# Three RMS norms with reciprocal root and scaled rows in PSUM, and the last chunk of two MLP first blocks with the contraction outermost

## The chip, the cores and the metric

The kernel runs on one core of one Trainium2 chip. The time is the device time of one execution in microseconds (us), read as the median of several executions. The engines are TensorE (PE in the rows, its weight loads PEld), VectorE (DVE), ScalarE (ACT), GpSimd (POOL) and SyncE (SP, here the queue that issues most DMAs). PSUM holds the results of matmuls: 8 banks of 128 partitions by 512 fp32 values.

## What is computed

A two-layer diffusion trunk on 1024 latent tokens and 256 context tokens of width 1024. Layer 0 mixes with a convolution and a Fourier transform, layer 1 with neighbourhood attention; each layer ends with a squared-ReLU MLP of width 4096. Ahead of every sub-layer stands an RMS norm with a shift and a scale:

```python
def _rms(x, g):
    y = x * lax.rsqrt(jnp.mean(x * x, axis=-1, keepdims=True) + EPS)
    return y * g
def _modulate(h, shift, scale):
    return h * (1 + scale) + shift
def _mlp(h, w1, w2):
    return jnp.square(jax.nn.relu(h @ w1)) @ w2
# per layer: x = x + gate1 * mixer(_modulate(_rms(x, g1), shift1, scale1))
#            x = x + gate2 * _mlp(_modulate(_rms(x, g2), shift2, scale2), w1, w2)
# ctx goes the same way with its own modulation (in the last layer it only feeds the attention)
```

## The kernel before

The token stream is kept transposed in SBUF as `xT[dt][ci]`: 8 blocks of 128 channels (`dt`) by 3 chunks of tokens (`ci`): chunks 0 and 1 are 512 latent tokens each, chunk 2 the 256 context tokens. Every dense product is done in three matmuls on numbers split into a high and a low part (`mm3`, L293 to L296): high by high, high by low, low by high. `dense` (L298) makes one block of 128 outputs for one chunk: 8 channel blocks `kt` by 3 matmuls, 24 in all, into one PSUM bank. `partial_groups` (L314) makes the output projections in groups of 6 or 12 matmuls; `residual` (L311, DVE) adds each group to `xT`, and `done` then squares the new block for the next norm.

The class `Norm` (L357) works in three steps. `square`: ACT squares each block (L369, L372) and DVE, or POOL where the caller says so, adds it to a sum in SBUF (L373). `stat`: a matmul with ones (L383) sums over the partitions, DVE takes mean plus epsilon out of PSUM (L386), ACT makes a first reciprocal root (L352) and DVE improves it in three instructions (L353 to L355); the result `y` is an SBUF tile named `ny`. `out`, once for each `dt`: on even blocks DVE forms x*g*y in an SBUF tile (L400), ACT adds the shift and writes the high part (L401), DVE the low part (L402); on odd blocks POOL multiplies x by y (L407), ACT does scale and shift (L405) and the copy to the high part (L406), DVE the low part (L408). The parts are called `mh`, `ml` ahead of the MLPs and `ah`, `al` ahead of the attention.

Three such norms are touched. I call their places **stage 1** (about 395 to 486 us, ahead of the first MLP), **stage 2** (about 1300 to 1375 us, ahead of the q, k, v projections, whose matmuls stand at L1152 to L1154) and **stage 3** (about 2005 to 2075 us, ahead of the second MLP). In each the norm of the chunk that is finished first is interleaved with the output projection of another chunk by `close_stream`, and the chunk that is finished last (`late`: chunk 0 in stage 1, chunk 1 in stage 3) gets its statistic and its eight `out` calls in the middle of the first block of the MLP (`mlp`, fc = 0): behind the first of the three dense groups of the chunk before it. The weights come by DMA as fp32 and are split into high and low by ACT (L247) and POOL or DVE (L248). The squared ReLU of an MLP group is L963 and L965 (ACT), L966 (POOL) and L967 (DVE).

All PSUM tiles come from one pool of 8 banks (`bank`). A scheduler assigns each tile a bank in the order in which the program asks for it, and orders the instructions of each engine; an engine waits where a tile's bank is not yet free.

Of the kernel before, what the change touches and what calls it, by code (L numbers as in the profile page):

```python
# [8 lines left out]
F32 = mybir.dt.float32  # L9
F32R = mybir.dt.float32r  # L10
BF16 = mybir.dt.bfloat16
AF = mybir.ActivationFunctionType
ALU = mybir.AluOpType
# [4 lines left out]
P = 128  # L18
D = 1024
DT = 8  # L20
# [3 lines left out]
EPS = 1e-6  # L24
CHUNKS = [(0, 512, 0), (512, 512, 0), (1024, 256, 1)]
# [11 lines left out]
def trunk(ctx: ExitStack, tc, x_t, cx_t, vecs, cc, ada, ada_t, w_in, w_out_2, w_fold, w_32, mlp_w1, mlp_w2, w_qkv, na_w_out_2, na_w_out_4, bias_pad,  # L37
# [4 lines left out]
    pp = ctx.enter_context(tc.tile_pool(name="pp", bufs=1))  # L42
# [20 lines left out]
    def bank():  # L63
        return psp.tile([P, 512], F32, tag="ps", name="ps")
# [64 lines left out]
    def tmp(dt=F32):  # L129
        return bp.tile([P, 512], dt, tag="tmp", name="tmp", bufs=ntmp[0])  # L130
# [219 lines left out]
    def rsqrt_newton(v, y, t):  # L350
# [3 lines left out]
                lambda: DVE.tensor_tensor(out=t, in0=t, in1=v, op=ALU.mult),  # L354
                lambda: DVE.scalar_tensor_tensor(out=y, in0=t, scalar=1.5, in1=y, op0=ALU.add, op1=ALU.mult)]  # L355

    class Norm:  # L357


        def __init__(self, l, k, hi, lo, room=None):  # L360
            self.l, self.k, self.hi, self.lo = l, k, hi, lo
            self.acc, self.y = {}, {}
            self.room = room or (lambda ci, which: keep())

# [14 lines left out]
        def stat_steps(self, ci, ps=None):  # L379
            w = CHUNKS[ci][1]  # L380
            if ps is None:
                ps = bank()
                PE.matmul(ps[:, :w], lhsT=ones, rhs=self.acc[ci][:, :w], start=True, stop=True)  # L383
            v, y, t = (a[:, :w] for a in (tmp(), self.room(ci, 1), tmp()))
            self.y[ci] = y
            return [lambda: DVE.tensor_scalar(out=v, in0=ps[:, :w], scalar1=1.0 / D, scalar2=EPS, op0=ALU.mult, op1=ALU.add)] + rsqrt_newton(v, y, t)  # L386
# [5 lines left out]
        def out_steps(self, dt, ci, on_dve=None):  # L392
            off, w, s = CHUNKS[ci]
            g = gtile[self.l][self.k][:, dt, s:s + 1]
            sh = mods[self.l][:, 24 * self.k + dt, s:s + 1]
            x, y, a = xT[dt][ci], self.y[ci], tmp()[:, :w]
            hs = self.hi[dt][:, off:off + w]
            ls = self.lo[dt][:, off:off + w]
            if dt % 2 == 0 if on_dve is None else on_dve:
                return (lambda: DVE.scalar_tensor_tensor(out=a, in0=x, scalar=g, in1=y, op0=ALU.mult, op1=ALU.mult),  # L400
                        lambda: ACT.activation(hs, a, AF.Identity, bias=sh),  # L401
                        lambda: DVE.scalar_tensor_tensor(out=ls, in0=a, scalar=sh, in1=hs.bitcast(F32), op0=ALU.add, op1=ALU.subtract))  # L402

            def high():
                ACT.activation(a, a, AF.Identity, bias=sh, scale=g)  # L405
                ACT.copy(hs, a)  # L406
            return (lambda: POOL.tensor_tensor(out=a, in0=x, in1=y, op=ALU.mult), high,  # L407
                    lambda: DVE.tensor_tensor(out=ls, in0=a, in1=hs.bitcast(F32), op=ALU.subtract))  # L408
# [458 lines left out]

    m_hi = [big(f"mh{d}") for d in range(DT)]
    m_lo = [big(f"ml{d}") for d in range(DT)]
    norm = Norm(0, 1, m_hi, m_lo)  # L870

    sequence(0, 0)
    sequence(1, 0)
# [72 lines left out]
        for t in todo:  # L946
            t()

    gs = partial_groups(y_hi[2:4], y_lo[2:4], 0, 0, (0,), 2, done=lambda m, ci: norm.square(m, ci, POOL if m % 2 else DVE))
    close_stream(gs[:4], gs[4:], (1,), norm)  # L950


    def mlp(l, norm, cis, late, fill, end, nf=8):
# [1 line left out]
        hh, hl = norm.hi, norm.lo  # L955

        def up(pcs, ci, uh, ul, between=None):
            off, w, _ = CHUNKS[ci]
            ps = dense(pcs, ci, hh, hl)
            if between:  # L960
                between()
            r, q = tmp(), tmp()
            ACT.activation(r[:, :w], ps[:, :w], AF.Relu)  # L963
            hs = uh[:, off:off + w]
            ACT.activation(hs, r[:, :w], AF.Square)  # L965
            POOL.tensor_tensor(out=q[:, :w], in0=r[:, :w], in1=r[:, :w], op=ALU.mult)  # L966
            DVE.tensor_tensor(out=ul[:, off:off + w], in0=q[:, :w], in1=hs.bitcast(F32), op=ALU.subtract)  # L967

        order = [ci for ci in cis if ci != late] + [late]
        for fc in range(nf):  # L970
# [3 lines left out]
            if fc == 0:  # L974
                pcs = take()
                pcs += [w for a in plan.pop(0) for w in pieces(*a, lambda: big("wq")[:, 0:1024])]
                for n, ci in enumerate(order):
                    for i in range(3):
                        w = pcs[2 * i:2 * i + 2]
                        if (n, i) == (1 - l, 0):  # L980
                            up(w, ci, uh[i], ul[i], lambda: norm.stat(late))
                            norm.all_out(late)
                        else:
                            up(w, ci, uh[i], ul[i])
                f = 3
            while f < 4:
                pcs = take()
# [11 lines left out]

    a_hi = []  # L1000
    a_lo = []
    norm1 = Norm(1, 0, a_hi, a_lo)

    def end0(uh, ul):
        a_hi.extend(big(f"ah{d}") for d in range(DT))
# [313 lines left out]
    for i in range(len(seq) + 3):  # L1319
# [21 lines left out]
        if 3 <= i:  # L1341
# [7 lines left out]
    slot[0], ntmp[0] = NLAT, 5  # L1349
    m_hi = [big(f"mh{d}") for d in range(DT)]  # L1350
    m_lo = [big(f"ml{d}") for d in range(DT)]
    norm = Norm(1, 1, m_hi, m_lo)
    close_stream(partial_groups(o_hi[6:], o_lo[6:], 1, 0, (0,), 2, done=norm.square, lag=3),
                 partial_groups(o_hi[4:], o_lo[4:], 1, 0, (1,), 4, done=lambda m, ci: norm.square(m, ci, POOL if m % 2 else DVE)), (0,), norm, wait=2)

# [299 lines left out]
```

## Time and profile before

| what | us |
|---|---|
| median of 3 runs | 2735.89 (2733.70 to 2740.11) |
| the profiled execution, its own time | 2737.96 |
| its span in the trace | 2736.1 |
| PE busy in the span | 2638.0 |

The profiled execution lies 2.1 us above the median. PE is busy for 96% of the span, so the time is read as PE's busy time plus PE's idle time, and the question for each stage is what PE waits for there and at which clock it runs afterwards.

### The profile page before, as it was taken

What the parts mean: (1) busy time and instruction counts of PE and PEld (TensorE: products, weight loads), DVE (VectorE), ACT (ScalarE), POOL (GpSimd) and SP (SyncE); (2) the same over time, 40 slices, a digit from 0 to 9 for tenths busy, and PEclk for the clock granted to TensorE, in tenths of its full rate; (3) what the DMA queues carried; (4) which work ended last, traced back from release to release, by engine and by line L of the source; (5) the groups of instructions that cost most, each with busy time, mean ns of one, the idle gap of its engine ahead of it and who ended that gap; (6) DMA issues with size and microseconds to landing.
All of it is one profiled execution on the core that took longest, in us unless ns stands there. A gap on an engine that the chain in (4) does not pass through costs nothing.

```text
span 2736.1 us, 37282 instructions
## 1 busy us (share of the span) xinstructions
PE 2638.0 (96%) x13787; PEld 2186.3 (80%) x13787; DVE 1665.2 (61%) x3623; ACT 913.9 (33%) x1988; POOL 1017.1 (37%) x838
## 2 busy tenths in 40 slices
PE   7989799999999999999899999999989899999999
PEld 5878687888888888888688887788868778788787
DVE  5778779455464554624962535888877645545545
ACT  4211246121221211213532225766744232232322
POOL 3323256332332322323411002544466454454543
PEclk9999899999999999999999999999999999999999
DMA  7233420222222222311333334534221111111112
GB/s 251 72 115 124 132 82 16 63 92 81 81 96 73 85 84 78 97 43 46 97 119 116 122 118 138 166 101 136 92 66 39 39 60 48 47 55 39 62 46 85
DMA packets 148937, 239.44 MB, mean 88 GB/s; under 512 B 10460, under 2 KB 91644, under 8 KB 148756
## 3 DMA queue, kind: packets, MB, share of 16 engines
q1 hardware_dynamic: 147316, 234.45, 26.8%
q8 instruction: 108, 1.77, 0.3%
q10 hardware_dynamic: 1440, 2.62, 0.2%
q14 instruction: 73, 0.60, 0.1%
HBM read 208.71 MB, written 28.32 MB: 87 GB/s over the span
## 4 chain that ended last, share of the span: by engine, by line
PE 72%; DVE 9%; issue 3%; DMA 2%; POOL 2%; ACT 1%; DVEq 0%; POOLq 0%; SPq 0%; ACTq 0%
PE ps L295 16%; PE ps L294 16%; PE ps L296 16%; PE ps L1464 5%; PE ps L1152 3%; PE ps L1154 3%; PE ps L1153 3%; PE ps L102 3%; PE ps L1288 3%; DMA raw<-in_mlp_w_dram 2%; PE ps L1105 2%; DVE junk L218 1%; POOL wsp L248 1%; PE ps L1107 1%; DVE ny L373 1%
## 5 line engine op out<-in xcount | busy, mean ns | idle before, releaser
L248 POOL TENSOR_TENSOR wsp<-raw,wsp 128x512 fp32r<-128x512 f32 x355 | 500.0, 1413 | 938.0 <-ACT wsp L247 904.4
L311 DVE SCALAR_TENSOR_TENSOR xT<-ps,mods,xT 128x512 f32<-128x512 f32 x528 | 367.0, 711 | 308.8 <-PE ps L296 308.3
L247 ACT CAST wsp<-raw 128x512 fp32r<-128x512 f32 x368 | 224.5, 619 | 758.6 <-PE ps L296 538.7
L295 PE MATMUL ps<-ul,wsp 128*128 128x512 f32 (+1 forms) x1280 | 473.5, 370 | 1.7 <-DVE ul L1470 0.8
L218 DVE CUSTOM_DVE_ANT_0 junk<-raw,cond_b 128x256 bf16<-128x256 f32 x640 | 354.8, 554 | 192.6 <-DMA raw<-in_ada_t_dram 92.7
L296 PE MATMUL ps<-uh,wsp 128*128 128x512 f32 (+1 forms) x1280 | 468.4, 368 | 0.0
L294 PE MATMUL ps<-uh,wsp 128*128 128x512 f32 (+1 forms) x1280 | 458.9, 369 | 0.5 <-ACT wsp L247 0.5
L295 PE MATMUL ps<-ml,wsp 128*128 128x512 f32 (+1 forms) x792 | 285.5, 361 | 11.1 <-DVE ml L408 7.5
L294 PE MATMUL ps<-mh,wsp 128*128 128x512 f32 (+1 forms) x792 | 284.6, 361 | 1.2 <-ACT mh L401 1.2
L296 PE MATMUL ps<-mh,wsp 128*128 128x512 f32 (+1 forms) x792 | 283.7, 359 | 0.0
L295 PEld LDWEIGHTS ps<-ul,wsp 128*128 128x128 f32 x1280 | 241.4, 189 | 47.0 <-DVE ul L1470 7.2
L294 PEld LDWEIGHTS ps<-uh,wsp 128*128 128x128 f32 x1280 | 241.4, 189 | 41.9 <-ACT wsp L247 0.9
L296 PEld LDWEIGHTS ps<-uh,wsp 128*128 128x128 f32 x1280 | 241.2, 188 | 40.0
L966 POOL TENSOR_TENSOR tmp<-tmp 128x512 f32<-128x512 f32 (+1 forms) x104 | 103.8, 999 | 217.8 <-ACT tmp L963 189.6
L295 PEld LDWEIGHTS ps<-ml,wsp 128*128 128x128 f32 x792 | 151.1, 191 | 37.4 <-DVE ml L408 10.8
L294 PEld LDWEIGHTS ps<-mh,wsp 128*128 128x128 f32 x792 | 151.0, 191 | 24.6 <-ACT mh L401 1.4
L296 PEld LDWEIGHTS ps<-mh,wsp 128*128 128x128 f32 x792 | 151.2, 191 | 21.4
L1464 PE MATMUL ps<-mh,wsp 128*128 128x512 f32 x448 | 148.1, 397 | 14.0 <-ACT ny L1481 7.2
L963 ACT ACTIVATE tmp<-ps 128x512 f32<-128x512 f32 (+1 forms) x104 | 55.3, 532 | 257.7 <-PE ps L296 257.2
L967 DVE TENSOR_TENSOR ul<-tmp,uh 128x512 fp32r<-128x512 f32 (+1 forms) x104 | 90.5, 875 | 80.8 <-POOL tmp L966 80.8
L294 PE MATMUL ps<-hh,wsp 128*128 128x512 f32 (+1 forms) x360 | 130.0, 361 | 1.9 <-ACT wsp L247 1.6
L295 PE MATMUL ps<-hl,wsp 128*128 128x512 f32 (+1 forms) x360 | 129.5, 360 | 2.0 <-DVE hl L408 1.3
(335 smaller groups left out, 5079.0 us busy)
## 6 DMA issues: line engine op xcount, KB each, us to landing
raw<-in_mlp_w_dram SPq DMA_DIRECT2D x92, 512.0 KB, 3.5
raw<-in_ada_t_dram SPq DMA_DIRECT2D x80, 512.0 KB, 3.5
raw<-in_mlp_w_dram SPq DMA_DIRECT2D x80, 256.0 KB, 2.7
raw<-in_w_qkv_dram SPq DMA_DIRECT2D x24, 512.0 KB, 4.0
k_d<-tmp SPq DMA_DIRECT2D x40, 256.0 KB, 2.4
kh<-k_d SPq DMA_DIRECT2D x15, 640.0 KB, 5.0
kl<-k_d SPq DMA_DIRECT2D x15, 640.0 KB, 6.9
araw<-in_ada_dram SPq DMA_DIRECT2D x16, 512.0 KB, 9.6
```

Of the source, the lines that this page charges most:

```text
L102: PE.transpose(dst, src, ident[:rows, :rows])
L218: DVE.tensor_tensor_reduce(out=junk, in0=raw[:, d * 256:d * 256 + 256], in1=cond_b[:, s, :], op0=ALU.mult, op1=ALU.add, scale=1.0, scalar= ...
L247: ACT.copy(dst_hi, src)
L248: lo_eng.tensor_tensor(out=dst_lo, in0=src, in1=dst_hi.bitcast(F32), op=ALU.subtract)
L294: PE.matmul(ps, lhsT=whi, rhs=ahi, start=first, stop=False)
L295: PE.matmul(ps, lhsT=whi, rhs=alo, start=False, stop=False)
L296: PE.matmul(ps, lhsT=wlo, rhs=ahi, start=False, stop=last)
L311: DVE.scalar_tensor_tensor(out=xT[dt][ci], in0=ps, scalar=mods[l][:, 24 * k + 16 + dt, s:s + 1], in1=xT[dt][ci], op0=ALU.mult, op1=ALU.add)
L966: POOL.tensor_tensor(out=q[:, :w], in0=r[:, :w], in1=r[:, :w], op=ALU.mult)
L967: DVE.tensor_tensor(out=ul[:, off:off + w], in0=q[:, :w], in1=hs.bitcast(F32), op=ALU.subtract)
L1152: PE.matmul(ps, lhsT=ah, rhs=wh, start=(kt == 0), stop=False)
L1464: PE.matmul(ps, lhsT=a, rhs=b, start=(first and kt == 0 and n == 0), stop=(kt == 3 and n == 2), skip_group_check=True)
```

## The change

The three norms get `psum=True`. Their statistic then goes straight from the PSUM bank of the ones matmul into ACT (scale 1/D, bias from a new tile `eps`, L391 of the changed kernel), DVE needs three instructions (L392 to L394) and not four, and `y` is written to a PSUM bank. Each `out` takes the DVE form for all eight blocks; x*g*y goes to a PSUM bank (L411), ACT reads it there (L412), DVE makes the low part (L413). POOL no longer multiplies (L407) or adds squares (L373). In the first block of both MLPs the late chunk runs its three dense groups together, in three open banks, with `kt` in the outer loop; the three squared ReLUs follow.

```diff
+    eps = pp.tile([P, 1], F32, name="eps")
+    POOL.memset(eps, EPS)
...
+            if self.psum:
+                y, y0, t = bank()[:, :w], tmp()[:, :w], tmp()[:, :w]
+                self.y[ci] = y
+                return [lambda: ACT.activation(y0, ps[:, :w], AF.Abs_reciprocal_sqrt, scale=1.0 / D, bias=eps),
+                        lambda: DVE.scalar_tensor_tensor(out=t, in0=y0, scalar=-0.5 / D, in1=y0, op0=ALU.mult, op1=ALU.mult),
+                        lambda: DVE.scalar_tensor_tensor(out=t, in0=ps[:, :w], scalar=D * EPS, in1=t, op0=ALU.add, op1=ALU.mult),
+                        lambda: DVE.scalar_tensor_tensor(out=y, in0=t, scalar=1.5, in1=y0, op0=ALU.add, op1=ALU.mult)]
...
-            x, y, a = xT[dt][ci], self.y[ci], tmp()[:, :w]
+            x, y, a = xT[dt][ci], self.y[ci], (bank if self.psum else tmp)()[:, :w]
...
-            if dt % 2 == 0 if on_dve is None else on_dve:
+            if self.psum or (dt % 2 == 0 if on_dve is None else on_dve):
...
-    norm = Norm(0, 1, m_hi, m_lo)
+    norm = Norm(0, 1, m_hi, m_lo, psum=True)
...
-    gs = partial_groups(y_hi[2:4], y_lo[2:4], 0, 0, (0,), 2, done=lambda m, ci: norm.square(m, ci, POOL if m % 2 else DVE))
+    gs = partial_groups(y_hi[2:4], y_lo[2:4], 0, 0, (0,), 2, done=norm.square)
...
-                for n, ci in enumerate(order):
+                w = [pcs[2 * i:2 * i + 2] for i in range(3)]
+                for n, ci in enumerate(order[:-1]):
                     for i in range(3):
-                        w = pcs[2 * i:2 * i + 2]
                         if (n, i) == (1 - l, 0):
-                            up(w, ci, uh[i], ul[i], lambda: norm.stat(late))
+                            up(w[i], ci, uh[i], ul[i], lambda: norm.stat(late))
                             norm.all_out(late)
                         else:
-                            up(w, ci, uh[i], ul[i])
+                            up(w[i], ci, uh[i], ul[i])
+                open_ = [None] * 3
+                for kt in range(DT):
+                    for i in range(3):
+                        open_[i] = dense(w[i], late, hh, hl, (kt, kt + 1), open_[i])
+                for i in range(3):
+                    squared_relu(open_[i], late, uh[i], ul[i])
...
-    norm1 = Norm(1, 0, a_hi, a_lo)
+    norm1 = Norm(1, 0, a_hi, a_lo, psum=True)
...
-    norm = Norm(1, 1, m_hi, m_lo)
+    norm = Norm(1, 1, m_hi, m_lo, psum=True)
...
-                 partial_groups(o_hi[4:], o_lo[4:], 1, 0, (1,), 4, done=lambda m, ci: norm.square(m, ci, POOL if m % 2 else DVE)), (0,), norm, wait=2)
+                 partial_groups(o_hi[4:], o_lo[4:], 1, 0, (1,), 4, done=norm.square), (0,), norm, wait=2)
```

Where the scheduler puts the instructions is seen in two places. The numbers in a row are the tiles'; a row's wait names the engine whose count is waited for. The first place is DVE in stage 1 from the statistic of the late chunk 0 on (`ul` is a low part of the MLP's squared ReLU, `g01` the norm's gain). Before:

```order
L386 TENSOR_SCALAR tmp_3821<-ps_3819 128x512 [waits DVE_49,PE_49]
L967 TENSOR_TENSOR ul_3675<-tmp_3789,uh_3671 128x256 [waits Activation_49,Pool_49]
L353 SCALAR_TENSOR_TENSOR tmp_3823<-ny_3822 128x512 [waits Activation_49]
L354 TENSOR_TENSOR tmp_3823<-tmp_3823,tmp_3821 128x512 [waits DVE_49]
L355 SCALAR_TENSOR_TENSOR ny_3822<-tmp_3823,ny_3822 128x512 [waits DVE_49]
L400 SCALAR_TENSOR_TENSOR tmp_3835<-xT0_84,g01_78,ny_3822 128x512 [waits DVE_49]
L967 TENSOR_TENSOR ul_3673<-tmp_3830,uh_3669 128x512 [waits Activation_49,Pool_49]
L400 SCALAR_TENSOR_TENSOR tmp_3844<-xT0_84,g01_78,ny_3822 128x512
L402 SCALAR_TENSOR_TENSOR ml0_2917<-tmp_3835,mods0_75,mh0_2909 128x512 [waits Activation_49]
```

And in the changed kernel, of which the same engine's rows there are:

```order
L392 SCALAR_TENSOR_TENSOR tmp_3815<-tmp_3814 128x512 [waits DVE_49,Activation_49]
L393 SCALAR_TENSOR_TENSOR tmp_3815<-ps_3811,tmp_3815 128x512 [waits DVE_49]
L394 SCALAR_TENSOR_TENSOR ps_3813<-tmp_3815,tmp_3814 128x512 [waits DVE_49]
L981 TENSOR_TENSOR ul_3665<-tmp_3821,uh_3661 128x512 [waits Activation_49,Pool_49]
L411 SCALAR_TENSOR_TENSOR ps_3826<-xT0_84,g01_78,ps_3813 128x512 [waits DVE_49]
L411 SCALAR_TENSOR_TENSOR ps_3830<-xT0_84,g01_78,ps_3813 128x512
L411 SCALAR_TENSOR_TENSOR ps_3834<-xT0_84,g01_78,ps_3813 128x512
L411 SCALAR_TENSOR_TENSOR ps_3838<-xT0_84,g01_78,ps_3813 128x512
L411 SCALAR_TENSOR_TENSOR ps_3842<-xT0_84,g01_78,ps_3813 128x512
L411 SCALAR_TENSOR_TENSOR ps_3846<-xT0_84,g01_78,ps_3813 128x512
L411 SCALAR_TENSOR_TENSOR ps_3850<-xT0_84,g01_78,ps_3813 128x512
L413 SCALAR_TENSOR_TENSOR ml0_2919<-ps_3826,mods0_75,mh0_2911 128x512 [waits Activation_49]
```

Seven L411 now stand ahead of the first low part, each with a PSUM tile of its own, where before one L400 alternated with low parts and wrote SBUF; the eighth L411 takes the bank of the first. With `y` (ps_3813) these are eight PSUM tiles, and the next row of DVE behind the last shown makes `ml1` out of ps_3830.

The second place is PE at the same point, where behind the statistic (L383, L387) the second dense group of chunk 1 begins. Before, that group (ps_3871) begins with no wait:

```order
L296 MATMUL ps_3794<-mh6_2915,wsp_3682 128x512
L383 MATMUL ps_3819<-ny_3544,ones_71 128x512 [waits Pool_49]
L294 MATMUL ps_3871<-mh0_2909,wsp_3687 128x512
L295 MATMUL ps_3871<-ml0_2917,wsp_3687 128x512
L296 MATMUL ps_3871<-mh0_2909,wsp_3687 128x512
```

In the changed kernel the group is ps_3858:

```order
L295 MATMUL ps_3786<-ml7_2926,wsp_3674 128x512 [waits DVE_49]
L296 MATMUL ps_3786<-mh7_2918,wsp_3674 128x512
L387 MATMUL ps_3811<-ny_3541,ones_71 128x512 [waits DVE_49]
L294 MATMUL ps_3858<-mh0_2911,wsp_3679 128x512 [waits DVE_49]
L295 MATMUL ps_3858<-ml0_2919,wsp_3679 128x512
```

It now waits for a count of DVE, because the bank that it got is the one of ps_3830: in the built program the count is the one that DVE reaches with `ml1` (L413), the last reader of ps_3830. The group that follows waits for `ml2` and the three open groups of the late chunk for `ml3` to `ml5`.

The third place is PE in stage 1 behind the statistic of chunk 1, inside the output projection of chunk 0 (groups of 6 matmuls, `yh` and `yl` the mixer's output). Before:

```order
L383 MATMUL ps_3590<-ny_3315,ones_71 128x512 [waits DVE_49]
L294 MATMUL ps_3609<-yh_1401,wsp_3269 128x512
...
L294 MATMUL ps_3633<-yh_1401,wsp_3533 128x512 [waits Activation_49]
L295 MATMUL ps_3633<-yl_1402,wsp_3533 128x512
L296 MATMUL ps_3633<-yh_1401,wsp_3533 128x512 [waits Pool_49]
...
L294 MATMUL ps_3658<-yh_1401,wsp_3533 128x512
```

In the changed kernel:

```order
L387 MATMUL ps_3587<-ny_3317,ones_71 128x512 [waits DVE_49]
L294 MATMUL ps_3604<-yh_1403,wsp_3271 128x512
...
L294 MATMUL ps_3627<-yh_1403,wsp_3530 128x512 [waits DVE_49]
L295 MATMUL ps_3627<-yl_1404,wsp_3530 128x512
L296 MATMUL ps_3627<-yh_1403,wsp_3530 128x512 [waits Pool_49]
...
L294 MATMUL ps_3650<-yh_1403,wsp_3530 128x512 [waits DVE_49]
```

Of the three groups behind the statistic the second now waits for L393 (it takes the statistic's bank) and the third for `ml2`. DVE's queue between them holds four adds of squares (L377), L392 to L394, five L411, `ml0`, one L311, `ml1` and `ml2`.

## Rows read from the trace of the kernel before

**Rows 1.** Page, part 1: busy time of each engine over the span.

```profile
PE 2638.0 (96%) x13787; PEld 2186.3 (80%) x13787; DVE 1665.2 (61%) x3623; ACT 913.9 (33%) x1988; POOL 1017.1 (37%) x838
```

**Rows 2.** Waits of PE, whole span: who waits for whom, us, times, longest.

```profile
PE ps L295 <- DVE ml L408: 7.5, 4, 2.4
...
PE ps L383 <- DVE ny L373: 4.1, 1, 4.1
PE ps L295 <- DVE ml L402: 3.6, 3, 2.1
```

**Rows 3.** Busy time by stretch (us of each engine, instructions), then granted PE clock.

```profile
core 0: us, PE busy (x) PEld busy (x) DVE busy (x) ACT busy (x) POOL busy (x), PEclk, DMA share, GB/s
443.00:455.00 12.00, 8.85 (x19) 6.07 (x20) 10.14 (x12) 9.15 (x17) 8.48 (x7) 0.50 0.00 0
456.00:486.00 30.00, 30.00 (x141) 24.96 (x140) 22.61 (x22) 17.37 (x29) 19.44 (x14) 1.00 0.07 18
486.00:1320.00 834.00, 834.00 (x4354) 718.50 (x4353) 431.03 (x1087) 179.42 (x325) 256.59 (x216) 1.00 0.24 77
1366.00:1370.00 4.00, 3.17 (x10) 2.69 (x11) 3.91 (x10) 3.13 (x6) 0.00 (x0) 0.57 0.09 27
2018.00:2022.00 4.00, 3.61 (x7) 2.19 (x8) 2.51 (x5) 2.54 (x3) 0.00 (x0) 0.57 0.38 131
```

**Rows 4.** PE in order of time, stage 1, chunk 1 (start, length, idle before, releaser).

```profile
439.03 0.28 PE L296 MATMUL ps<-mh,wsp 128*128 128x256 f32 x1
...
443.14 0.79 PE L295 MATMUL ps<-ml,wsp 128*128 128x512 f32 x1 [2.10 <-DVE ml L402]
...
455.43 1.02 PE L383 MATMUL ps<-ny,ones 128*128 128x512 f32 x2
...
456.98 0.39 PE L294 MATMUL ps<-mh,wsp 128*128 128x512 f32 x1
457.21 0.39 PE L295 MATMUL ps<-ml,wsp 128*128 128x512 f32 x1
```

**Rows 5.** DVE and POOL in order of time, stage 1, output projection.

```profile
419.06 0.67 DVE L919 TENSOR_TENSOR xT<-xT,tmp 128x512 f32<-128x512 f32 x1
419.66 0.41 DVE L408 TENSOR_TENSOR ml<-tmp,mh 128x256 fp32r<-128x256 f32 x1
...
423.59 0.74 DVE L311 SCALAR_TENSOR_TENSOR xT<-ps,mods,xT 128x512 f32<-128x512 f32 x1
424.25 1.12 DVE L373 TENSOR_TENSOR ny<-ny,tmp 128x512 f32<-128x512 f32 x1
423.34 1.48 POOL L248 TENSOR_TENSOR wsp<-raw,wsp 128x512 fp32r<-128x512 f32 x1
```

**Rows 6.** DVE and ACT in order of time behind the statistic of chunk 0.

```profile
456.49 0.69 DVE L386 TENSOR_SCALAR tmp<-ps 128x512 f32<-128x512 f32 x1 [0.60 <-PE ps L383]
457.21 0.63 ACT L352 ACTIVATE ny<-tmp 128x512 f32<-128x512 f32 x1 [2.54 <-DVE tmp L386]
...
458.61 0.69 DVE L354 TENSOR_TENSOR tmp<-tmp 128x512 f32<-128x512 f32 x1
459.33 0.69 DVE L355 SCALAR_TENSOR_TENSOR ny<-tmp,ny 128x512 f32<-128x512 f32 x1
```

**Rows 7.** PE in order of time, stage 2: the first and the last of its six stalls.

```profile
1330.18 0.50 PE L1153 MATMUL ps<-wsp,ah 128*128 128x512 f32 x1 [1.52 <-POOL wsp L248]
...
1366.83 1.12 PE L102 MATMUL ps<-ident,ny 128*128 128x128 f32 x4 [3.69 <-DVE ny L1190]
```

**Rows 8.** PE and DVE in order of time, stage 3.

```profile
2018.39 1.96 PE L383 MATMUL ps<-ny,ones 128*128 128x512 f32 x2 [4.08 <-DVE ny L373]
2049.09 1.91 PE L383 MATMUL ps<-ny,ones 128*128 128x512 f32 x2
2024.63 0.68 DVE L355 SCALAR_TENSOR_TENSOR ny<-tmp,ny 128x512 f32<-128x512 f32 x1
2044.56 1.77 DVE L402 SCALAR_TENSOR_TENSOR ml<-tmp,mods,mh 128x512 fp32r<-128x512 f32 x1
```

More of the change, by code (lines that the diff above doesn't have):

```diff
@@ L355, in rsqrt_newton, with __init__ @@
                 lambda: DVE.scalar_tensor_tensor(out=y, in0=t, scalar=1.5, in1=y, op0=ALU.add, op1=ALU.mult)]
+    eps = pp.tile([P, 1], F32, name="eps")
+    POOL.memset(eps, EPS)
     class Norm:
-        def __init__(self, l, k, hi, lo, room=None):
-            self.l, self.k, self.hi, self.lo = l, k, hi, lo
+        def __init__(self, l, k, hi, lo, room=None, psum=False):
+            self.l, self.k, self.hi, self.lo, self.psum = l, k, hi, lo, psum
             self.acc, self.y = {}, {}
@@ L957, in up @@
         def up(pcs, ci, uh, ul, between=None):
-            off, w, _ = CHUNKS[ci]
             ps = dense(pcs, ci, hh, hl)
@@ L961, in up, with squared_relu @@
                 between()
+            squared_relu(ps, ci, uh, ul)
+        def squared_relu(ps, ci, uh, ul):
+            off, w, _ = CHUNKS[ci]
             r, q = tmp(), tmp()
```

## The prediction

> **What bounds the kernel now.** I read the page's busy times first: PE works for 2638 us of a span of 2736 [rows 1], so a change of the norms can only act through PE's idle time and PE's clock. The view of PE's waits then says who holds PE in the three stages: low parts that DVE makes (`ml`, from L408 and L402, 7.5 and 3.6 us), the last add of squares ahead of the ones matmul (4.1 us) [rows 2], and in stage 2 split weights and the transposes of q and k [rows 7]. Between the stages there is nothing to win and nothing to hide a loss: from 456 to 486 us and from 486 to 1320 us PE is busy without a gap at full clock [rows 3]. A microsecond lost in stage 1 is a microsecond on the end.
>
> After a gap the clock counts too. A 512-column matmul follows the last in 0.227 us at full clock [rows 4]; from 443 to 455 us, behind the gaps of chunk 1, the granted clock is 0.50, the lower of its two levels, 1.2 GHz. Behind the 4.1 us gap of stage 3 it is 0.57 on average over 2018 to 2022, behind the 3.7 us gap of stage 2 0.57 over 1366 to 1370 [rows 3]: four microseconds at 0.57 lose 4 x 0.43 = 1.7 us. I take 1.7 us for every gap of 3 us or more.
>
> What the three stages lose now: in stage 1 the last matmul of chunk 2 starts at 439.03 and the statistic of chunk 0 at 455.43 [rows 4]; between lie 24 matmuls, 24 x 0.227 = 5.4 us, so 16.3 - 5.5 = 10.8 us go to four gaps and the low clock. In stage 2 the six gaps add up to 9.6 us (1.5 the first, 3.7 the last [rows 7]), with the low clock 11. In stage 3 it is 4.1 ahead of the first statistic, then 2.1, 0.7, 2.4 and 0.7 for low parts, and about 5 of low clock (the second statistic takes 1.9 us where it takes 1.0 at full clock [rows 4, 8]): 15. Together 37 us, the most that the change could bring.
>
> **The change part by part.** *What gets cheaper.* POOL multiplies no more, and DVE's instructions with an operand in PSUM should not be drawn out: L402, all in SBUF, takes 1.77 us in stage 3 beside POOL [rows 8], L311, which reads PSUM, takes 0.74 in the middle of a POOL instruction of 1.48 [rows 5]. The chain from statistic to `y` loses one DVE instruction, 0.7 us. Weight splits on POOL start sooner.
>
> *What gets dearer: banks.* All tiles of a norm's output now come from the 8 banks that PE needs for its groups, and the order in which the program asks for them decides. The rows of the changed order show the second group behind the statistic of chunk 0 waiting for DVE's `ml1`; nothing of that kind stood there.
>
> *Stage 1, late chunk.* I count from the start of the ones matmul. DVE reads its result 1.06 us later (456.49 - 455.43) [rows 4, 6], so ACT can too. ACT's root takes 0.63 [rows 6] and ends at 1.7. L392, L393, L394 each need the one before: 0.72 apart as L354 and L355 are [rows 6], so `y` is there at 3.9. Then DVE's queue has one low part of the squared ReLU (L981, 0.6), ends 4.5. Then seven L411, `ml0`, `ml1`. No instruction of before has DVE write PSUM; the nearest row is L311, 0.74 long and followed 0.66 later by the next [rows 5]. Bounds: 0.60 below (two instructions with all operands in SBUF, 419.06 and 419.66 [rows 5]), 0.9 above (half-way from 0.66 to the 1.12 of an add drawn out by POOL [rows 5], as if the write too met a second user). I take 0.66, the row with the same kind of operand: 9 x 0.66 = 5.9, and the last one's completion 0.1: `ml1` ends at 10.5. PE has finished the ones matmul at 0.9. PE waits 9.6 us and loses 1.7 to the clock: **+11.3** (10.2 to 13.5). Before, this same stretch was hidden: two more dense groups of chunk 1 ran over it [rows 3].
>
> *Stage 1, chunk 1.* Here the gain is real: the low parts of chunk 1 are done before its dense group begins, so the 10.8 us go. But PE is held inside the output projection instead. Behind the statistic of chunk 1 DVE has four adds of squares, all now its own and with both operands in SBUF (1.12 beside POOL [rows 5], 0.7 without; I take 1.05), two L311, L392 and L393: 4 x 1.05 + 4 x 0.66 = 6.9 us, of which PE's ones matmul and its one group of 6 matmuls cover 0.9 + 1.4: 4.6 us of gap. The next group waits for `ml2`: L394, five L411, `ml0`, L311, `ml1`, `ml2` = 10 x 0.66 = 6.6, less its own 1.4: 5.2 more. DVE also comes to this place about 1 us later, since it took over half of chunk 2's outputs. With the clock 4.6 + 5.2 + 1 + 1.7 = 12.5 us against 10.8: **+2** (-2.5 to +4).
>
> *Stage 2.* One bank wait of about 1.6 us (the third group of the projection waits for the first low part, 7.9 us behind the statistic, and has two groups of 12, 2.7 us each, and the statistic's own 0.9 ahead of it). The waits for weights shrink from 4.7 to about 1.2, since POOL has only the weights to do; the 3.7 us gap goes because DVE is ahead there; 1 us of short transposes stays, and some low clock. About 4.5 against 11: **-6.5** (-10 to -3).
>
> *Stage 3.* The first statistic still waits about 4 us for the last add of squares: one add that POOL did is now DVE's, against less contention. `y` comes some 1.3 us sooner than L355's end at 2025.3 [rows 8]; the third group then waits for `ml0`, about 1 to 2 us. Chunk 0's dense group runs without gaps and ends near 2041.5, where before the second statistic stood at 2049.1 [rows 8]. But that statistic now needs the adds of chunk 1, five on DVE after the last groups: near 2043.7. Then the late chain of stage 1 again, 10.5 us to `ml1`: PE goes on at 2054.2 and has lost the clock, as if at 2055.9. Before, it went on at 2050.0 with 1.2 us of low clock to come: 2051.2. **+4.5** (+1 to +8).
>
> *At nothing.* The late chunk with `kt` outermost: its stalls are meant to vanish, but it had none [rows 3], and 72 matmuls are 72 matmuls. Cover gone, it could cost the three squared ReLUs at its end, which the fourth dense block, 13 us, hides. The memset of `eps` lies at the start. The attention between stages 2 and 3 is reordered in a few dozen rows, with no more work.
>
> Sum: 11.3 + 2 - 6.5 + 4.5 = +11.3 on the profiled execution's 2738.0, that is 2749.3; the median of before lies 2.1 below it: **2747 us**, +0.4%.
>
> One rule of the Trainium skill speaks against the change, and it stands behind the row of 456 to 486 us, where nothing waits because the norm's tiles are in SBUF: Perfetto Trace Analysis, section Matmuls, wants independent groups to rotate through different banks so that evacuation of one overlaps the next. By it alone I could not size the loss; the sum above does not use it. Another would move the sum. Beside the L402 of 1.77 us, SBUF — State Buffer, section Who interferes with whom, says that a VectorE instruction with at most one SBUF input does not contend with GpSimd. By that rule no L411 or L413 is drawn out, which is the sum above; without it, L413 at 1.77 would add 1.1 to each of the two low parts on every late chain, +2.2 twice, 2751.
>
> **The rivals.** *A, relief* (not slower). Place: the adds of squares and POOL's weight splits in stages 1 and 3. With POOL off the norms, the adds take 0.7 instead of 1.12 and the splits end sooner. Price: four adds ahead of L393, 4 x 0.4 = 1.6 us, and the 1 us by which DVE comes late; five adds in stage 3, 2; its first statistic 2 earlier; stage 2 at its lower end, 3.5: -10, so 2737. It decides once adds cost under 0.8 us. For it: POOL loses all its multiplications of these norms, beside which L402 took 1.77 us [rows 8]. Against: POOL's weight splits stay, and 1.12 is from a stretch where POOL did splits [rows 5].
>
> *B, as meant* (faster). PE's bank waits come out at half, because DVE's chain of L411 with its operands in PSUM runs at 0.4 us each and the adds are cheap as in A: 9 x 0.26 in each late chain and 10 x 0.26 in chunk 1, 7.3 on top of A: 2730. Against: the shortest step behind 512 columns that I show is 0.60 [rows 5].
>
> *C, PSUM writes are dear.* An L411 that reads and writes PSUM at 0.9: 9 x 0.24 twice, 10 x 0.24 in chunk 1, 6 x 0.24 in stage 2: +8, 2755.
>
> *D, the change does not hold PE at all.* The order of banks does not hold PE, and all 37 us go: 2700. The order's rows speak against it: the wait is written there.
>
> **How the numbers follow.** My forecast, slower by 6 to 16 us, 0.5; C and worse 0.16; A 0.22; B 0.1; D 0.02. About 0.2% of the time, 5.5 us, is what a measurement of this kernel can tell from no change: under 2730.4 is faster, over 2741.4 slower. Slower 0.66, within 0.22, faster 0.12. The range from A's better half to C: 2731 to 2759.
>
> **What would show it.** Right: PE idle for 8 to 11 us behind the L387 of each late chunk (stages 1 and 3), released by DVE's L413; two gaps of about 5 us in 425 to 442; no gap on `ml` in chunk 1's first group; the gap of 3.7 us in stage 2 gone. Wrong: L411 apart by much less or more than 0.66; adds at 0.7; PE running on behind the late statistic; a stage 2 as slow as before.

## The result, and the profile after

The changed kernel takes 2755.18 us (median of 6 runs, 2751.02 to 2758.34) against 2735.80 (6 runs) for the kernel before: ratio 1.0067, 95% interval 1.0057 to 1.0078, slower by 19.4 us. The forecast was 2747 with a range of 2731 to 2759. The sign and the main mechanism, PE held by banks behind the two late statistics, were right; the size was not: 11 us forecast, 19 measured, from two places treated below (stage 2 and the attention). The profiled execution of the changed kernel has 2758.34 us and a span of 2756.5, 20.4 more than the span of before.

PE is as busy as before, so on balance the 20 us are idle time of PE (span less busy: 98.1 us before, 119.0 now); the new stretches of low clock stand against old ones that went:

```profile
PE 2637.5 (96%) x13787; PEld 2190.1 (79%) x13787; DVE 1643.8 (60%) x3655; ACT 894.9 (32%) x1956; POOL 953.4 (35%) x799
```

The row answers to [rows 1]: PE 2637.5 us against 2638.0, POOL 64 us less. Who holds PE now, in the view of its waits (us in total, times, longest):

```profile
PE ps L294 <- DVE ml L413: 26.4, 4, 9.5
...
PE ps L102 <- DVE p L1157: 12.3, 4, 5.4
...
PE ps L387 <- DVE ny L377: 7.2, 3, 3.8
```

In [rows 2] the waits for low parts stood at L295, the matmul that reads the low part, and came to 11 us. Now 26 us stand at L294, the first matmul of a group, which reads only the high part: such a wait for L413 is not one for the number but for the bank that L413 was the last to read. The row in the middle belongs to the attention, where the same wait came to 7.7 us before; the prediction took it as unchanged.

To see where the 20.4 us arise I matched the instructions of DVE in the two traces, each with its counterpart of the same operation, names and shape, and took the median difference of their starts where it stands still between the stages.

| kernel (profiled execution) | ahead of stage 1 | stage 1 | stage 2 | attention | stage 3 |
|---|---|---|---|---|---|
| forecast | 0 | +13.3 | -6.5 | 0 | +4.5 |
| the change | +1.2 | +13.5 | -2.2 | +4.5 | +3.5 |
| `outs_later` | +0.9 | +2.4 | -1.8 | -1.6 | -6.0 |
| `kt_inner` | -0.9 | +13.3 | -2.3 | +2.2 | +5.0 |
| `a_in_sbuf` | -0.4 | +1.7 | -6.1 | +6.0 | -7.8 |
| `kt_outer_only` | -0.2 | -0.9 | +1.3 | -2.2 | -1.5 |
| `stage1_only` | -1.9 | +12.0 | -0.1 | -0.1 | -0.1 |
| `stage2_only` | +0.8 | -0.1 | -2.3 | +2.3 | -0.1 |
| `stage3_only` | -1.0 | +0.5 | 0.0 | -0.1 | +4.9 |
| `pool_squares` | -1.7 | +14.3 | -2.4 | +4.7 | +6.2 |
| `stages23_sbuf` | -0.1 | -1.1 | -2.7 | -1.5 | -8.2 |
| `stages23_y_sbuf` | -1.1 | -0.1 | -0.5 | +0.2 | -3.8 |

Each column is us against the kernel before. The first column has no part of the change beyond a memset; with `kt_outer_only`, whose stages 2 and attention do no other work than before, it shows that one execution against another differs by 1 to 2 us in a column. Each row is a single execution; the medians given with the experiments are the firmer numbers. Stage 1 was forecast to the microsecond, stage 3 within one. What is missing is 4.3 us of gain in stage 2 and 4.5 us in the attention.

The gaps of the changed kernel in order of time: stage 1 (the first five rows), stage 2 (four), stage 3 (four). The columns are start, length, and in brackets the idle time ahead with what ended it:

```profile
429.13 2.07 PE L387 MATMUL ps<-ny,ones 128*128 128x512 f32 x2 [2.43 <-DVE ny L377]
435.27 0.50 PE L294 MATMUL ps<-yh,wsp 128*128 128x512 f32 x1 [2.08 <-DVE tmp L393]
442.06 0.80 PE L294 MATMUL ps<-yh,wsp 128*128 128x512 f32 x1 [4.29 <-DVE ml L413]
459.43 1.02 PE L387 MATMUL ps<-ny,ones 128*128 128x512 f32 x2
469.94 0.80 PE L294 MATMUL ps<-mh,wsp 128*128 128x512 f32 x1 [9.49 <-DVE ml L413]
...
1329.52 0.50 PE L294 MATMUL ps<-uh,wsp 128*128 128x512 f32 x1 [2.01 <-DVE al L413]
1348.25 0.50 PE L1172 MATMUL ps<-wsp,ah 128*128 128x512 f32 x1 [0.74 <-ACT wsp L247]
1350.75 0.79 PE L1173 MATMUL ps<-wsp,ah 128*128 128x512 f32 x1 [2.00 <-POOL wsp L248]
1380.92 0.66 PE L102 MATMUL ps<-ident,ny 128*128 128x128 f32 x4 [1.56 <-DVE ny L1210]
...
2035.11 1.13 PE L387 MATMUL ps<-ny,ones 128*128 128x512 f32 x2 [3.78 <-DVE ny L377]
2044.76 0.50 PE L294 MATMUL ps<-oh,wsp 128*128 128x512 f32 x1 [3.04 <-DVE ml L413]
2059.63 1.12 PE L387 MATMUL ps<-ny,ones 128*128 128x512 f32 x2 [0.97 <-DVE ny L377]
2070.30 0.80 PE L294 MATMUL ps<-mh,wsp 128*128 128x512 f32 x1 [9.55 <-DVE ml L413]
```

Beside [rows 4] the gaps on `ml` at L295 are gone: chunk 1's first group runs through and the late statistic stands at 459.43 where it stood at 455.43, although the groups ahead of it were held for 8.8 us. Then PE does nothing but the ones matmul for ten microseconds. What DVE does meanwhile answers to [rows 6] (start, length; x7 is seven in a row):

```profile
461.21 0.69 DVE L392 SCALAR_TENSOR_TENSOR tmp<-tmp 128x512 f32<-128x512 f32 x1 [5.44 <-ACT tmp L391]
461.94 0.69 DVE L393 SCALAR_TENSOR_TENSOR tmp<-ps,tmp 128x512 f32<-128x512 f32 x1
462.66 0.70 DVE L394 SCALAR_TENSOR_TENSOR ps<-tmp 128x512 f32<-128x512 f32 x1
463.27 0.68 DVE L981 TENSOR_TENSOR ul<-tmp,uh 128x512 fp32r<-128x512 f32 x1
463.87 4.70 DVE L411 SCALAR_TENSOR_TENSOR ps<-xT,g,ps 128x512 f32<-128x512 f32 x7
468.48 2.72 DVE L413 SCALAR_TENSOR_TENSOR ml<-ps,mods,mh 128x512 fp32r<-128x512 f32 x4
```

Four steps of about 0.7, seven of 0.66 (463.87 to 468.48), two low parts, and PE goes on at 469.94, 10.5 us behind the start of the ones matmul. That is the chain of the prediction, number by number.

The clock, by stretches of ten microseconds (busy time of each engine, instructions, then the granted PE clock):

```profile
430.00:440.00 10.00, 5.70 (x14) 3.23 (x12) 9.83 (x15) 4.92 (x9) 2.01 (x2) 0.67 0.07 27
440.00:450.00 10.00, 7.94 (x45) 7.36 (x46) 10.00 (x17) 5.36 (x10) 2.59 (x3) 0.70 0.10 26
470.00:480.00 10.00, 10.00 (x37) 8.16 (x38) 5.28 (x8) 1.92 (x3) 1.04 (x1) 0.83 0.00 0
1325.00:1335.00 10.00, 7.99 (x29) 6.11 (x28) 9.96 (x16) 6.03 (x10) 1.55 (x2) 0.83 0.17 59
1345.00:1355.00 10.00, 7.26 (x25) 5.33 (x24) 9.93 (x14) 5.71 (x13) 6.00 (x5) 0.83 0.61 197
...
2032.00:2060.00 28.00, 20.88 (x87) 16.30 (x88) 25.21 (x34) 14.76 (x24) 11.97 (x8) 1.00 0.28 85
```

From 470 to 480 PE is busy throughout at 0.83, which is 10 x 0.17 = 1.7 us lost, what [rows 3] gave. In stage 2 the same 0.83 stands behind gaps of only 2.0 us, and in stage 3 the clock stays at 1.00 through gaps of 3.78 and 3.04 us. So the length of a gap does not say by itself whether the clock falls. The same gap can go either way: `outs_later`, a run of the next section, has the first of the two in stage 2 as well (2.00 us, ending at 1318.10), with the same work around it, and there the clock does not fall:

```profile
1313.00:1323.00 10.00, 8.00 (x35) 6.29 (x34) 9.93 (x16) 5.94 (x10) 2.31 (x2) 1.00 0.22 75
```

### The profile page after: what moved, and what is told of

Read it like the earlier page. It is cut to its first block, busy times and chain, and to the rows that moved or that the text cites. A ratio compares the mean times of both kernels' runs of the same rounds, so it can differ in the third digit from the quotient of the medians.

```text
span 2756.5 us, 37266 instructions
## 1 busy us (share of the span) xinstructions
PE 2637.5 (96%) x13787; PEld 2190.1 (79%) x13787; DVE 1643.8 (60%) x3655; ACT 894.9 (32%) x1956; POOL 953.4 (35%) x799
## 4 chain that ended last, share of the span: by engine, by line
PE 73%; DVE 9%; issue 3%; DMA 2%; POOL 2%; ACT 1%; SPq 0%; DVEq 0%; POOLq 0%; ACTq 0%
PE ps L294 16%; PE ps L295 16%; PE ps L296 16%; PE ps L1484 5%; PE ps L1173 4%; PE ps L1174 4%; PE ps L1172 3%; PE ps L102 3%; PE ps L1308 3%; DMA raw<-in_mlp_w_dram 2%; PE ps L1125 2%; DVE junk L218 1%; POOL wsp L248 1%; PE ps L1127 1%; DVE ps L411 1%
## 5 line engine op out<-in xcount | busy, mean ns | idle before, releaser
L311 DVE SCALAR_TENSOR_TENSOR xT<-ps,mods,xT 128x512 f32<-128x512 f32 x528 | 366.8, 711 | 304.1 <-PE ps L296 303.5
L295 PE MATMUL ps<-ul,wsp 128*128 128x512 f32 (+1 forms) x1280 | 474.1, 370 | 1.2 <-DVE ul L1490 0.2
L294 PE MATMUL ps<-uh,wsp 128*128 128x512 f32 (+1 forms) x1280 | 459.8, 370 | 2.5 <-DVE al L413 2.0
L294 PE MATMUL ps<-mh,wsp 128*128 128x512 f32 (+1 forms) x792 | 284.4, 359 | 19.0 <-DVE ml L413 19.0
L295 PE MATMUL ps<-ml,wsp 128*128 128x512 f32 (+1 forms) x792 | 284.0, 359 | 0.0
L295 PEld LDWEIGHTS ps<-ul,wsp 128*128 128x128 f32 x1280 | 241.9, 189 | 46.7 <-DVE ul L1490 6.7
L294 PEld LDWEIGHTS ps<-uh,wsp 128*128 128x128 f32 x1280 | 241.9, 189 | 44.4 <-DVE al L413 2.4
L294 PEld LDWEIGHTS ps<-mh,wsp 128*128 128x128 f32 x792 | 151.1, 191 | 42.5 <-DVE ml L413 20.7
L295 PEld LDWEIGHTS ps<-ml,wsp 128*128 128x128 f32 x792 | 151.0, 191 | 21.5
L981 DVE TENSOR_TENSOR ul<-tmp,uh 128x512 fp32r<-128x512 f32 (+1 forms) x104 | 82.8, 802 | 114.5 <-POOL tmp L980 84.8
L294 PE MATMUL ps<-hh,wsp 128*128 128x512 f32 (+1 forms) x360 | 130.0, 361 | 2.3 <-ACT wsp L247 1.8
L295 PE MATMUL ps<-hl,wsp 128*128 128x512 f32 (+1 forms) x360 | 129.8, 361 | 2.0 <-DVE hl L419 1.3
```

The source lines that it names most:

```text
L294: PE.matmul(ps, lhsT=whi, rhs=ahi, start=first, stop=False)
L295: PE.matmul(ps, lhsT=whi, rhs=alo, start=False, stop=False)
L311: DVE.scalar_tensor_tensor(out=xT[dt][ci], in0=ps, scalar=mods[l][:, 24 * k + 16 + dt, s:s + 1], in1=xT[dt][ci], op0=ALU.mult, op1=ALU.add)
```

## The experiments

**Is it the order in which banks are asked for?** The changed kernel with the eight `out` calls of the late chunk moved behind the three groups of the chunk before it:

```diff
                         if (n, i) == (1 - l, 0):
                             up(w[i], ci, uh[i], ul[i], lambda: norm.stat(late))
-                            norm.all_out(late)
                         else:
                             up(w[i], ci, uh[i], ul[i])
+                norm.all_out(late)
                 open_ = [None] * 3
```

> The changed kernel with one thing moved: the eight out calls of the late chunk stand behind the three dense groups of the chunk before it, not behind the first, so that those groups get their banks first. Theory (banks are given in program order and the norm's tiles take them all): the two gaps of 9.5 us behind the late statistics go, with 1.7 us of low clock each, so 2 x 11 = 22 us less than the changed kernel, about 2733 us. Rival (DVE, which now does POOL's half too, is simply too late with the low parts): the gaps move to the late chunk's groups, at most half of the 22 us comes back, 2744 or more.

It takes 2730.12 us, ratio to before 0.9978 (0.9969 to 0.9988): 25 us less than the changed kernel, a little more than the 22 expected, and 6 us faster than before. The stretches around its late statistics (459.36 in stage 1, 2044.52 in stage 3), columns as above:

```profile
455.00:480.00 25.00, 25.00 (x110) 20.30 (x110) 14.85 (x23) 10.66 (x17) 4.54 (x5) 1.00 0.00 1
2040.00:2050.00 10.00, 7.68 (x32) 5.74 (x31) 7.13 (x11) 3.67 (x7) 3.78 (x3) 1.00 0.27 84
2050.00:2070.00 20.00, 20.00 (x90) 16.54 (x90) 10.95 (x17) 8.76 (x14) 4.62 (x4) 1.00 0.05 14
```

Behind both statistics PE has no gap, at full clock. The 2.3 us missing from 2040 to 2050 lie ahead of stage 3's statistic, which waits for the last add of squares and not for a bank:

```profile
2044.52 1.13 PE L387 MATMUL ps<-ny,ones 128*128 128x512 f32 x2 [2.32 <-DVE ny L377]
```

DVE does the same instructions, in nearly the same order, as in the changed kernel, and no gap reappears on low parts in the late chunk: the rival, that DVE is too late, is out for these two places. By the table the move gives back 11.1 us in stage 1 and 9.5 in stage 3; the rest of the 25 is the attention (+4.5 there, -1.6 here), of which below. So by these two executions some 21 us of the 25 come from the two late gaps, and the order in which the banks are asked for is their cause.

**Does the outermost contraction matter?** Two kernels: the change without it (the loop of before over all three chunks), and it alone on the kernel before.

```diff
-                for n, ci in enumerate(order[:-1]):
+                for n, ci in enumerate(order):
...
-                open_ = [None] * 3
-                for kt in range(DT):
-                    for i in range(3):
-                        open_[i] = dense(w[i], late, hh, hl, (kt, kt + 1), open_[i])
-                for i in range(3):
-                    squared_relu(open_[i], late, uh[i], ul[i])
```

> The changed kernel with the late chunk's three dense groups one after the other again (contraction innermost). Theory: the outermost contraction neither costs nor brings anything, since DVE is done with most low parts when the late chunk begins: within 3 us of the changed kernel, 2752 to 2758. Rival (the open groups hold three banks and that is part of the loss, or they hide waits for low parts): a difference of 5 us or more, either way.

> The kernel before with the contraction outermost in the late chunk of both first blocks, nothing else. Theory: nothing to gain, the late chunk had no gaps: within 3 us of before, 2733 to 2739. Rival (three open banks hold up PE or the squared ReLU that comes in one go): 5 us slower or more.

2755.34 us without it (ratio 1.0071, 1.0056 to 1.0086), 2735.76 with it alone (0.9999, 0.9989 to 1.0008). It does nothing either way, as the busy row of 456 to 486 in [rows 3] said: a chunk that never waits cannot gain from another order of its matmuls.

**Banks or the load on DVE?** The changed kernel with x*g*y in SBUF again; `y` stays in PSUM, all blocks stay on DVE.

```diff
-            x, y, a = xT[dt][ci], self.y[ci], (bank if self.psum else tmp)()[:, :w]
+            x, y, a = xT[dt][ci], self.y[ci], tmp()[:, :w]
```

> The changed kernel with x*g*y in SBUF tiles as before; the statistic's steps and y stay in PSUM, all eight blocks stay on DVE. Theory (banks): only one bank is taken, the late gaps and those inside the output projection of stage 1 go, and the gaps of before on low parts drawn out by POOL do not come back: 25 to 35 us less than the changed kernel, 2720 to 2730. Rival (the load on DVE is the loss): the gaps stay, now on low parts, and at most 10 us come back, 2745.

2728.72 us, 0.9975 (0.9966 to 0.9984): 26 us less than the change, with DVE doing just as many instructions. The load on DVE is not the loss. But the composition was not as I expected. Stage 3 goes from +3.5 to -7.8 and stage 2 from -2.2 to -6.1, close to what I had forecast for stage 2 (the section on the prediction says how much of that is the clock); stage 1 remains at +1.7, since a new wait takes the place of the bank waits in the output projection:

```profile
426.54 1.12 PE L387 MATMUL ps<-ny,ones 128*128 128x512 f32 x2 [1.57 <-DVE ny L377]
440.33 0.58 PE L294 MATMUL ps<-mh,wsp 128*128 128x256 f32 x1 [5.67 <-ACT wsp L247]
```

Chunk 2's dense group waits 5.7 us for its first weights, which ACT splits: a wait that did not exist before, in a stage where the old kernel lost 10.8.

**Are the serial adds on DVE to blame?** The odd squares back on POOL in stages 1 and 3:

```diff
-    gs = partial_groups(y_hi[2:4], y_lo[2:4], 0, 0, (0,), 2, done=norm.square)
+    gs = partial_groups(y_hi[2:4], y_lo[2:4], 0, 0, (0,), 2, done=lambda m, ci: norm.square(m, ci, POOL if m % 2 else DVE))
...
-                 partial_groups(o_hi[4:], o_lo[4:], 1, 0, (1,), 4, done=norm.square), (0,), norm, wait=2)
+                 partial_groups(o_hi[4:], o_lo[4:], 1, 0, (1,), 4, done=lambda m, ci: norm.square(m, ci, POOL if m % 2 else DVE)), (0,), norm, wait=2)
```

> The changed kernel with the odd squares added on POOL again, as before. Theory (banks): the waits for DVE's low parts stay; in stage 1 and 3 the last adds come 1 to 3 us sooner, since DVE has half of them, and the first gaps shrink by so much: 2750 to 2755. Rival (the serial adds on DVE are the loss): 8 us or more less than the changed kernel, 2747 or under.

2758.10 us, 1.0078 (1.0065 to 1.0092). Not even the 1 to 3 us that I expected came: stage 1 reads +14.3, stage 3 +6.2, and the late gaps are 9.5 us each as in the change. Rival A's adds are not the lever.

**Each stage alone**, on the kernel before, without the outermost contraction: `psum=True` in one of the three places (and, in stages 1 and 3, the squares on DVE).

> The kernel before with only stage 1's norm in PSUM, no kt-outermost loop. The attention's order is that of before on DVE. Theory: stage 1 costs 13 us, nothing else moves: 2749, one gap of 9.5 us behind the late statistic. Rival (the loss of stage 1 needs the three open banks of the late chunk): 2742 or less.

> The kernel before with only stage 2's norm in PSUM (statistic, y and x*g*y), no kt-outermost loop. Its attention is ordered nearly as in the changed kernel (5 places differ on DVE, against 69 from before). Theory (the attention lost its 4.5 us to the order of its rows, not to more work): stage 2 brings 2 us as in the changed kernel, attention costs 4 to 5: 2 to 3 us slower than before, 2738 to 2739, with PE waiting some 14 us for p in the attention. Rival (the attention's loss was a chance of one execution): attention within 2 us of before, total 2733 to 2734.

> The kernel before with only stage 3's norm in PSUM banks as changed, no kt-outermost loop; the attention's order is that of before but for 5 places on DVE. Theory: stage 3 costs 3.5 to 6 us as in the changed kernel and the run with squares on POOL, the attention nothing: 2739 to 2742, one gap of 9.5 us behind the late statistic. Rival (stage 3's loss comes from the changed attention ahead of it): 2737 or less.

Stage 1 alone: 2747.17 us, 1.0041 (1.0027 to 1.0054). Stage 3 alone: 2741.42, 1.0024 (1.0014 to 1.0034). Both as expected, each with one gap of 9.5 us, and by the table each leaves everything else where it was, within the 1 to 2 us by which executions differ. Stage 2 alone: 2737.50, 1.0000 (0.9991 to 1.0009), between the two expectations; its stage gains 2.3 us, as in the change, and the attention behind it takes 2.3 more. PE's waits in the attention of before, then of this kernel:

```profile
PE ps L102 <- DVE p L1137: 7.7, 4, 3.2
PE ps L102 <- ACT pT L1266: 0.9, 1, 0.9
```

```profile
PE ps L102 <- DVE p L1151: 12.7, 4, 5.5
PE ps L102 <- POOL p L1151: 2.0, 1, 2.0
```

`p` is the row of softmax weights that DVE or POOL scales (L1137 of before) ahead of its transposes; the waits for it are 14.7 us where they were 7.7. Where the time goes is seen at the longest of these waits, in the changed kernel:

```profile
1703.77 1.26 POOL L1323 TENSOR_TENSOR ol<-ou,oh 64x512 fp32r<-64x512 f32 x1 [3.27 <-DVE sums L1154]
1704.01 3.73 DVE L1157 TENSOR_SCALAR p<-p,sums 128x640 f32<-128x640 f32 x1
1705.01 0.80 POOL L1157 TENSOR_SCALAR p<-p,sums 128x640 f32<-128x640 f32 x1
1705.77 2.53 POOL L1063 TENSOR_TENSOR bm<-tb,maskt 128x384 f32<-128x384 f32 x3
1707.89 0.45 PE L102 MATMUL ps<-ident,p 128*128 128x128 f32 x1 [5.44 <-DVE p L1157]
```

and at its counterpart before:

```profile
1692.23 0.53 DVE L1137 TENSOR_SCALAR p<-p,sums 128x640 f32<-128x640 f32 x1
1692.91 0.85 PE L102 MATMUL ps<-ident,p 128*128 128x128 f32 x6 [1.89 <-DVE p L1137]
```

One scaling of `p` on DVE takes 3.73 us, where the median of its 63 rows is 0.55, and PE waits for it 3.5 us longer than before. The kernels sort by this row. The order of DVE's rows in the attention of the changed kernel differs from before in some 70 places; `stage2_only`, `kt_inner`, `a_in_sbuf` and `pool_squares` have that order too but for 0 to 5 places, in all five this one `p` takes 3.73 or 3.74 us, and the attention costs 2.2 to 6.0 us (mean 3.9). In the other six, whose order is that of before or a third one, no `p` takes more than 1.67 us, and the attention lies between -2.2 and +0.2. So most of the 4.5 us is one drawn-out instruction that the new order brings about. POOL works beside it without a pause; that this draws it out is likely but not shown, since in the rows of before `p` ran beside POOL's `ol` in 0.53. Stage 2's norm is enough to bring the order about (`stage2_only`) but does not fix it: `outs_later` has the same norm and the third order. Why the scheduler chose it is open.

**A version that beats both, and what `y` in PSUM is worth.** Stage 1 as before, stages 2 and 3 with the statistic and `y` in PSUM, x*g*y in SBUF, all on DVE, the outermost contraction kept; then the same with `y` in SBUF too:

```diff
-                y, y0, t = bank()[:, :w], tmp()[:, :w], tmp()[:, :w]
+                y, y0, t = self.room(ci, 1)[:, :w], tmp()[:, :w], tmp()[:, :w]
```

> Stage 1's norm as before; stages 2 and 3 with the statistic and y in PSUM, but x*g*y in SBUF tiles, all on DVE; kt-outermost kept. Theory: stage 2 brings 6 us and stage 3 7 to 8 (what the kernel with x*g*y in SBUF showed), stage 1 nothing: 12 to 14 us less than before, 2722 to 2724, or 4 to 6 less than that gain if the attention falls into the slow order, 2728. Rival (y in PSUM brings nothing, the gain of that kernel was the free POOL of stage 1): 2732 or more.

> As the run with stages 2 and 3 alone and x*g*y in SBUF, but y in SBUF as well: only the statistic is read in PSUM, all blocks on DVE, POOL out of the norm. The attention's order is that of before but for 5 places on DVE. Theory (an instruction of DVE with two SBUF tensors is drawn out by POOL's weight splits, one with y in PSUM is not): L411 rises from 0.74 to 0.9 us or more on average, stage 3 gains 5 to 7 us instead of 8; with the attention at 0 the total is 2726 to 2730. Rival (the gain is POOL's absence alone): L411 stays at 0.75, stage 3 at 8, total 2724 to 2726.

The first takes 2725.20 us, 0.9959 (0.9946 to 0.9971), 11 us faster than before and 30 faster than the change; expected were 2722 to 2724 or 2728. Stage 3 gives the 8 us, stage 2 only 2.7 of the 6, where the clock was low (below). The second takes 2733.34, 0.9994 (0.9984 to 1.0004), slower than I expected (2726 to 2730): stage 3 gives 3.8 and stage 2 0.5. The groups of x*g*y on DVE, first with `y` in PSUM, then with `y` in SBUF (busy us, mean ns of one):

```profile
L411 DVE SCALAR_TENSOR_TENSOR tmp<-xT,g,ps 128x512 f32<-128x512 f32 x32 | 22.8, 741 | 0.1
```

```profile
L411 DVE SCALAR_TENSOR_TENSOR tmp<-xT,g,ny 128x512 f32<-128x512 f32 x40 | 37.0, 948 | 0.9 <-DMA k_d<-tmp 0.7
```

741 ns against 948: the direction was right. The second group holds 8 rows of stage 1's old form as well, with a mean of 1115 ns; the 32 of stages 2 and 3 alone have 906. The two kernels differ by 8.1 us: by the table 4.4 in stage 3, 2.2 in stage 2 and 1.7 in the attention, whose order is that of before in the second and the third one in the first. The 0.165 us times 32 rows, 5.3 us on DVE, is of the size of the 6.6 in the two stages; how much of it PE waits for was not traced.

## Why the prediction was right or wrong

**The total.** The measured 2755 is the price of rival C, but that is chance: what C rested on, an L411 of 0.9 us, did not occur.

**Stage 1, late chunk: right.** `ml1` came 10.5 us behind the start of the ones matmul, PE waited 9.49 us (forecast 9.6), and the clock took 1.7. One L411, with `y` and its result in PSUM, starts 0.66 behind the other, so the value taken from L311 held, and rival C, dear PSUM writes, is out: the group's mean length is 750 ns with the result in PSUM and 740 with it in SBUF.

```profile
L411 DVE SCALAR_TENSOR_TENSOR ps<-xT,g,ps 128x512 f32<-128x512 f32 x48 | 33.1, 750 | 0.1
L413 DVE SCALAR_TENSOR_TENSOR ml<-ps,mods,mh 128x512 fp32r<-128x512 f32 x32 | 22.4, 745 | 0.2
```

The second row bears on the rule of the Trainium skill that the prediction weighed (SBUF — State Buffer, section Who interferes with whom, a VectorE instruction with at most one SBUF input does not contend with GpSimd). L413 with x*g*y in PSUM has a mean of 745 ns; in `a_in_sbuf`, and so with two SBUF inputs, 850; L411 with `y` in SBUF has 906 in stages 2 and 3. The trace agrees with the rule: with two SBUF inputs single rows take up to 1.78 us, with one none of these takes over 0.77.

**Stage 1, chunk 1: right in sum, in part by luck.** The statistic came later than before by 4.0 us, of which 1.2 lay ahead of the stage: +2.8 against +2. The three gaps were 2.4, 2.1 and 4.3 where I had 1, 4.6 and 5.2, and the low clock lasted longer than 1.7 us: 0.67 and 0.70 over twenty microseconds. The gaps were over-estimated by 2 us and the clock under-estimated, and the two errors cancel. (By its own rows the old loss of 10.8 us is 11.0: 455.43 - 439.03 is 16.4, less 24 x 0.227.)

**Stage 2: the mis-sized term.** Forecast -6.5, measured -2.2, and -1.8 to -2.4 in five kernels with the same form. Three parts failed. The waits for weights were 0.74 + 2.00 = 2.7 us and not 1.2: POOL's being rid of the norm did not bring the split weights forward by as much. The bank wait was 2.0 and not 1.6. And the clock: "1.7 us for every gap of 3 us or more" was the step that let stage 2 off (its sum leaves 0.7 us for the clock), whereas the clock fell to 0.83 over ten microseconds, 1.7 us, behind each of the two gaps of 2.0 us. The bank wait 2.0, the weights 2.7, the transposes of q and k 1.6 (L102 at 1380.92 above) and the clock twice 1.7 make 9.7 us of loss, where I had 4.5. The limit of 3 us had no ground: in the prediction's own row of 443 to 455 us the clock stood at 0.50 [rows 3] behind gaps of which the longest was 2.10 [rows 4]. Nor does every gap cost clock, as the stretches of the changed kernel's stage 3 and of `outs_later` show. How much that moves stage 2 is seen in the two kernels that have no bank wait there, first `a_in_sbuf`, then `stages23_sbuf`:

```profile
1325.00:1345.00 20.00, 15.79 (x65) 11.53 (x64) 20.00 (x29) 11.90 (x23) 10.44 (x6) 1.00 0.50 152
```

```profile
1325.00:1345.00 20.00, 14.30 (x45) 10.28 (x45) 17.63 (x30) 10.28 (x21) 7.87 (x6) 0.74 0.46 138
```

Their gaps in stage 2 add up to 5.0 and 5.7 us, yet the first gains 6.1 us, at full clock throughout, and the second 2.7. So the forecast value came in one execution at full clock; the term that was mis-sized most is the clock's, and of the 4.3 us that are missing the bank wait as such explains little.

**Stage 3: right.** First statistic 3.8 (4 forecast), the wait of the third group 3.0 (1 to 2), the late gap 9.55; +3.5 against +4.5 (2055.9 - 2051.2 is 4.7). The third group's wait was longer than forecast, and in this execution neither of the first two gaps cost clock.

**The attention: wrong.** "Reordered in a few dozen rows, with no more work" was costed at nothing. It costs 4.5 us, in rows that no part of the change touches. The step that failed is that equal work in another order waits equally long: in the new order one `p` on DVE takes 3.73 us and not 0.53, and PE waits for it 5.44 us and not 1.89. I named no cover for it, and had no bound.

**The rest.** The 1.2 us ahead of stage 1 have no cause in the change and are of the size by which single executions differ. The sum of 11.3 became 20.4 in the profiled execution: +4.3 stage 2, +4.5 attention, +1.2 ahead, -1 in stage 3. Rival A failed on its place: the adds did cost less than before (mean 922 ns of 42, against 1.09 us) and the bank waits stood anyway. B and D were out with the first late gap.

The other rule named there, to rotate independent groups through different banks (the Trainium skill, Perfetto Trace Analysis, section Matmuls), speaks of groups of matmuls only. Here the group that waits 9.49 us has another bank than the group before it; what held that bank was a tile of VectorE. The rule as it stands does not speak of that case, and no run here was made to test it with two groups in a row in one bank.

## What to carry to other kernels

Putting a chain of eight intermediate tiles into PSUM cost the engines that write and read them next to nothing here, but TensorE waits for the whole chain if a pool gives those tiles the banks ahead of the next groups: ask for the groups' banks first, or keep the intermediates in SBUF and put only the one operand in PSUM that spares VectorE its contention. When a wait stands at the first matmul of a group and names an instruction whose result that matmul does not read, it is a bank that it waits for. And when a scheduler orders the program, look at the order of the regions that the edit does not touch as well, and in the trace for single instructions far above their median there: they were over a fifth of the loss here.

## What had not been expected of the hardware

That the length of a gap says so little about the clock: behind each of the two gaps of 2.0 us in stage 2 the granted clock was 0.83 over ten microseconds, the same as behind the gap of 9.5 us, while in stage 3 of the same execution it stayed at 1.00 through gaps of 3.78 and 3.04 us, and in `outs_later` at 1.00 behind the first of the two gaps of 2.0 us. VectorE writing PSUM was no dearer than writing SBUF (750 against 740 ns for 128x512), which I had bounded up to 0.9 us. And one VectorE instruction of 128x640 with all operands in SBUF took 3.73 us, against a median of 0.55.
